# A unit's third and fourth sums, not its first and third, made by accumulating DMAs; a plain block ahead of the first unit; the first norm scaled by columns

## The chip, the cores and the metric

The kernel runs as one program on one core of a Trainium2 chip. Its engines each work through an instruction list of their own, in order, and wait for one another by semaphores: PE (matmuls and transposes), DVE (VectorE), ACT (ScalarE), POOL (GpSimd) and SP, which here only issues DMAs. The metric is the device time of one execution in microseconds (us).

## What is computed

Two layers of a transformer block on x of 256 rows by 1024 columns, float32. Each layer has a gated FFN with 2816 hidden columns, a mixer of three kinds of attention, and a second FFN; a norm stands ahead of each and a last one at the end.

```python
def rms_norm(x, gain):
    y = x * lax.rsqrt(jnp.mean(x * x, axis=-1, keepdims=True) + NORM_EPS)
    return y * gain

def swiglu(h, w_gate, w_up, w_down):
    a, u = h @ w_gate, h @ w_up
    return (jax.nn.silu(a) * u) @ w_down

for l in range(DEPTH):                                   # DEPTH = 2
    x = x + 0.5 * swiglu(rms_norm(x, ffn1_norm[l]), ffn1_w_gate[l], ffn1_w_up[l], ffn1_w_down[l])
    x = x + hybrid_mixer(rms_norm(x, mix_norm[l]), w_in[l], ...)
    x = x + 0.5 * swiglu(rms_norm(x, ffn2_norm[l]), ffn2_w_gate[l], ffn2_w_up[l], ffn2_w_down[l])
return rms_norm(x, final_norm)
```

The change touches the four FFNs (`f1` and `f2` of layers 0 and 1) and the first norm; the mixer stays as it is.

## The kernel before

**Precision.** Every float32 operand of a product is split in two: a high part, rounded by an ACT copy (`high`, L184), and a low part, the rest, by a DVE subtraction (`low`, L187). One product is three matmuls, high by high, high by low and low by high (`mm3`, L175 to L177). So each weight that arrives as `w_r`, `f_G_r` or `f_U_r` is read by ACT, then by DVE, before PE may use it as `w_h` and `w_l`. The normed and transposed x is `f_Th` and `f_Tl`.

**An FFN.** The hidden columns come as blocks of 128. The *first block* (`first_block`, L560) makes blocks 0 and 1 for both row tiles t of 128 rows, 48 matmuls of 128x256 each, gate and up together. When tile 1 begins, it lets DVE and ACT start on the four sums `f_Sh`, `f_Sl` of the quarters of x (`sums`, L614). Its result `f_f_b_h` (silu of gate times up, L554) is transposed on PE into `f_b0tp`. A *plain block* f (`block`, L589) is two steps, `g` and `u`, of 24 matmuls of 128x256 (`f_b`). Blocks 10 to 21 come as two *units* of six: there, gate (G) and up (U) are each computed as one Strassen-Winograd product of 2x2 quarters, with seven products in place of eight (`unit_product`, L641; 12 matmuls of 128x384 each, `f_s`). The seven come in the order `SEVEN`, 1, 5, 6, 3, 7, 2, 4. A *down* step of a block is 12 matmuls of 128x512 (`f_a`).

**The order.** `ffn_steps` (L473) writes one step of `FILL` after each of the 28 products of an FFN: `g` or `u` is half of a plain block, a number is the down step of that block. `REST` and the blocks left over follow. PE, ACT and DVE run in the order in which the program is written; `defer` puts an instruction off by a clock that the program keeps for itself. The order of the DMA issues on SP and POOL comes from the scheduler.

**Weights.** `load` (L307) issues a weight's DMA and its splits. Plain and down weights (512 KB) pass through `w_r`, a ring of 4608 columns, four such loads. A unit's quarter W00, W01, W10 or W11 of 128x4x384 (768 KB) has a tile in a pool of its own. Products 1, 2 and 3 take a quarter as it is (W00, W10, W11); the others take sums of quarters:

- product 5 takes a = W00 + W01: a load of W00 (a second one) and, once it has landed, a DMA from POOL that adds W01 to it in place (L318);
- product 6 takes a + W11, added by DVE in two halves (L344);
- product 7 takes b = W01 + W11, again a load and an accumulating DMA;
- product 4 takes a + W10 (with a as product 6 left it), added by DVE.

For each half of a unit these are 5 loads by SP, 2 accumulating DMAs and 2 adds on DVE. Unit weights are loaded only from the time that the first block is in its tile 1.

**A norm** (`norm`, L398). ACT squares and sums a half row tile (L422), DVE adds the halves (`f_ss`, L428), POOL makes r, one over the root (L429), DVE scales x by r and the gain into `f_xs` (L445), PE transposes that into `f_tp`, ACT makes `f_Th` from it and a second copy `f_xr` in SBUF (`kept`, L464), and DVE takes `f_Tl` from the copy. The sums of the units use the copy too. The first norm is different for tile 1: POOL multiplies x by the gain ahead of time (`f_xg`, L418). Its gain `first_g` is a DMA that writes the 1024 values to all 128 partitions (512 KB). At the start, `WARM` matmuls of zeros (`heat`) run on PE while the first loads are under way.

## Time and profile before

| | us |
|---|---|
| median of three runs | 1311.02 |
| lowest and highest of them | 1310.87, 1311.99 |
| the profiled execution, as timed | 1311.85 |
| its span in the profile | 1310.1 |
| PE busy | 1259.8 (96%) |
| DVE busy | 913.4 (70%) |
| ACT busy | 747.9 (57%) |
| POOL busy | 58.0 (4%) |

The DMAs read 257.95 MB in that span, 198 GB/s, of which the accumulating ones are 25.17 MB. A row of the profile names the line of the kernel, the engine, the operation, and `out<-in` with the names of the tiles; buffer numbers are left out, and `f_` stands for the tiles of all four FFNs. What follows in brackets is the time that the engine stood idle before the instruction, and what ended it. In the table of waits, the figures are the total, the number of times and the longest.

### The profile page before, as it was taken

To read this page: it belongs to the slowest core of one execution; us is meant where nothing else is said; L and a number is where in the kernel's file an instruction comes from. 1 tells how busy PE (TensorE), PEld (TensorE's weight loads), DVE (VectorE), ACT (ScalarE), POOL (GpSimd) and SP (SyncE) were. 2 spreads that over 40 slices of the span, in tenths; PEclk is the share of its full clock that TensorE was granted. 3 is DMA by queue.
4 is the path that set the end of the run, shared out by engine and by line. 5 is a ranking of instruction groups with operands and counts; after the bars stand their busy time and mean duration, and the time that the engine had idled before them with its cause. 6 is when DMAs were issued, how large, how long until landed. Compare 5 with 4: busy or idle time off the path is not lost.

```text
span 1310.1 us, 21172 instructions
## 1 busy us (share of the span) xinstructions
PE 1259.8 (96%) x8280; PEld 1183.3 (90%) x8280; DVE 913.4 (70%) x1354; ACT 747.9 (57%) x1267; POOL 58.0 (4%) x56
## 2 busy tenths in 40 slices
PE   7799999999999989999969999999999999799998
PEld 6799988999999879999869999899999998799996
DVE  5678776765556758797658797677655476688884
ACT  5566656665555546565446565466654654565652
POOL 1000001000000010000000000000000000100000
PEclk8899999999999999999999999999999999899999
DMA  9999755545435678994598994565464466999932
GB/s 282 282 279 263 206 190 162 167 129 147 129 107 178 213 237 215 264 289 154 177 274 210 267 280 158 178 190 150 130 161 121 127 190 177 258 264 271 265 127 82
DMA packets 214885, 260.38 MB, mean 199 GB/s; under 512 B 7425, under 2 KB 198657, under 8 KB 214785
## 3 DMA queue, kind: packets, MB, share of 16 engines
q1 hardware_dynamic: 197600, 233.34, 57.7%
q0 software_dynamic: 16896, 25.17, 11.6%
q8 instruction: 65, 1.06, 0.3%
q10 hardware_dynamic: 288, 0.52, 0.1%
q14 instruction: 36, 0.29, 0.1%
HBM read 257.95 MB, written 1.05 MB: 198 GB/s over the span
## 4 chain that ended last, share of the span: by engine, by line
PE 90%; DMA 5%; DVE 3%; ACT 2%; issue 1%; POOL 0%; SPq 0%; POOLq 0%; DVEq 0%; ACTq 0%
PE f_a L176 6%; PE f_a L177 6%; PE f_a L175 6%; PE f_s L175 6%; PE f_s L177 6%; PE f_s L176 6%; PE f_b L176 5%; PE f_b L175 5%; PE f_b L177 5%; DMA f_G_r<-in_ffn_w_gate 4%; PE mx_ogate L175 4%; PE mx_ogate L176 3%; PE mx_ogate L177 3%; PE mx_odqk L175 2%; PE mx_odqk L177 2%; PE mx_odqk L176 2%
## 5 line engine op out<-in xcount | busy, mean ns | idle before, releaser
L187 DVE TENSOR_TENSOR w_l<-w_r,w_h 128x512 fp32r<-128x512 f32 (+1 forms) x484 | 387.4, 826 | 104.9 <-ACT w_h L184 103.3
L184 ACT ACTIVATE w_h<-w_r 128x512 fp32r<-128x512 f32 (+1 forms) x484 | 344.8, 735 | 94.7 <-PE f_a L176 16.6
L175 PE MATMUL f_b<-f_Th,w_h 128*128 128x256 f32 x512 | 148.4, 290 | 0.0
L176 PE MATMUL f_b<-f_Th,w_l 128*128 128x256 f32 x512 | 148.0, 289 | 0.0
L177 PE MATMUL f_b<-f_Tl,w_h 128*128 128x256 f32 x512 | 147.7, 288 | 0.0
L175 PE MATMUL f_a<-w_h,f_hTh 128*128 128x512 f32 x352 | 139.5, 396 | 0.0
L177 PE MATMUL f_a<-w_l,f_hTh 128*128 128x512 f32 x352 | 139.0, 395 | 0.0
L176 PE MATMUL f_a<-w_h,f_hTl 128*128 128x512 f32 x352 | 138.9, 395 | 0.0
L184 ACT ACTIVATE w_h<-f_G_r 128x1536 fp32r<-128x1536 f32 (+1 forms) x72 | 85.6, 1197 | 60.7 <-DVE f_G_r L344 29.1
L187 DVE TENSOR_TENSOR w_l<-f_U_r,w_h 128x1536 fp32r<-128x1536 f32 (+1 forms) x72 | 100.4, 1399 | 20.1 <-ACT w_h L184 19.9
L175 PE MATMUL mx_ogate<-mx_Th,w_h 128*128 128x256 f32 x384 | 113.0, 294 | 0.0
L176 PE MATMUL mx_ogate<-mx_Th,w_l 128*128 128x256 f32 x384 | 108.6, 283 | 0.6 <-DVE w_l L187 0.6
L187 DVE TENSOR_TENSOR w_l<-f_G_r,w_h 128x1536 fp32r<-128x1536 f32 (+1 forms) x72 | 100.0, 1398 | 12.3 <-ACT w_h L184 11.5
L177 PE MATMUL mx_ogate<-mx_Tl,w_h 128*128 128x256 f32 x384 | 108.5, 283 | 0.0
L184 ACT ACTIVATE w_h<-f_U_r 128x1536 fp32r<-128x1536 f32 (+1 forms) x72 | 85.7, 1196 | 36.0 <-DVE f_U_r L344 22.1
L176 PEld LDWEIGHTS f_b<-f_Th,w_l 128*128 128x128 f32 x512 | 101.1, 197 | 0.2
L177 PEld LDWEIGHTS f_b<-f_Tl,w_h 128*128 128x128 f32 x512 | 101.1, 197 | 0.0
L175 PEld LDWEIGHTS f_b<-f_Th,w_h 128*128 128x128 f32 x512 | 101.1, 197 | 0.0
L175 PE MATMUL f_s<-w_h,f_Sh 128*128 128x384 f32 x256 | 87.2, 341 | 0.0
L177 PE MATMUL f_s<-w_l,f_Sh 128*128 128x384 f32 x256 | 86.6, 338 | 0.0
L176 PE MATMUL f_s<-w_h,f_Sl 128*128 128x384 f32 x256 | 86.6, 338 | 0.0
L177 PEld LDWEIGHTS f_a<-w_l,f_hTh 128*128 128x128 f32 x352 | 66.1, 188 | 15.8
(265 smaller groups left out, 2933.5 us busy)
## 6 DMA issues: line engine op xcount, KB each, us to landing
w_r<-in_ffn_w_down SPq DMA_DIRECT2D x88, 512.0 KB, 4.3
w_r<-in_w_in SPq DMA_DIRECT2D x84, 512.0 KB, 3.9
f_G_r<-in_ffn_w_gate SPq DMA_DIRECT2D x40, 768.0 KB, 8.1
f_U_r<-in_ffn_w_up SPq DMA_DIRECT2D x40, 768.0 KB, 7.3
w_r<-in_ffn_w_gate SPq DMA_DIRECT2D x40, 512.0 KB, 5.7
w_r<-in_ffn_w_up SPq DMA_DIRECT2D x40, 512.0 KB, 6.8
f_G_r<-in_ffn_w_gate POOLq DMA_DIRECT2D x16, 768.0 KB, 10.1
f_U_r<-in_ffn_w_up POOLq DMA_DIRECT2D x16, 768.0 KB, 10.2
```

The costliest lines, as they stand in the source:

```text
L175: nc.tensor.matmul(o, sh, mh, start=first, stop=False, skip_group_check=again)
L176: nc.tensor.matmul(o, sl, mh, start=False, stop=False, skip_group_check=again)
L177: nc.tensor.matmul(o, sh, ml, start=False, stop=last, skip_group_check=again)
L184: nc.scalar.activation(hi, src, AF.Copy)
L187: nc.vector.tensor_tensor(lo, src, hi.bitcast(F32), op=ALU.subtract)
```

## The change

- **Unit weights.** The four quarters are each loaded once: a = W00, b = W01, c = W11, d = W10. Product 1 takes a. For product 5 DVE adds b to a, for product 6 DVE adds c to a. Behind product 6's issue an accumulating DMA adds W11 to b, which is then product 7's; behind product 3's an accumulating DMA adds W10 to a, which is then product 4's. Products 3 and 2 take c and d. Per half of a unit: 4 loads by SP, 2 accumulating DMAs, 2 adds on DVE.
- **Order.** `LEAD` puts both steps of plain block 2 ahead of product 1 of the first unit; `FILL` and `REST` are shifted to make up for it. The work is the same in all.
- **First norm.** The gain comes as 8 rows of 128 (`gain_rows`); PE transposes them behind the heat, DVE copies the result to `gain_cols` (128x8). x is scaled by r alone, and DVE multiplies by the gain after the transposes, which leaves `f_xr` in SBUF; `f_Th` and `f_Tl` are made from that. The DMA of `first_g` and POOL's `f_xg` are gone; the DMAs of the gain and of `ident` are issued by ACT.
- **Other FFN norms.** `f_Tl` is taken from the transposes in PSUM, and ACT's copy for the sums is made later.
- `WARM` is 9 instead of 6.

```diff
-FILL = "gugu0 1gu2 3gu4 g", "u5 gu10 11 gu12 13 gu14 15 "
-REST = 6, 7, 8, 9
+LEAD = "gu"
+FILL = "gu0 1 gu2 3 gu4 5 gu", "gu6 gu7 10 gu11 12 13 14 15"
+REST = 8, 9
 FIRST, SINGLE, UNIT0 = 2, 8, 10
 SLOPES = [2.0 ** (-8.0 * (i + 1) / N_ALIBI) for i in range(N_ALIBI)]
 CHUNK = 1024
 PIECE = 512
 SCR = 2048
 ORDERED = {mybir.EngineType.PE, mybir.EngineType.Activation, mybir.EngineType.DVE}
-WARM = 6
+WARM = 9
 RING = 6656
 RAW = 4608
 PACE = 2.3 / 1024
...
-    def transpose(o, src):
-        nc.tensor.transpose(o, src, ident)
+    def transpose(o, src, n=P):
+        nc.tensor.transpose(o, src, ident[:n, :n])
         spend(0.11)
...
-    steps = {1: ((("q1", (0, 0)),), None, "q1"), 5: ((("a", (0, 0), (0, 1)),), None, "a"), 6: ((("q2", (1, 1)),), ("a", "q2"), "a"),
-             3: ((), None, "q2"), 7: ((("b", (0, 1), (1, 1)),), None, "b"), 2: ((("q3", (1, 0)),), None, "q3"), 4: ((), ("a", "q3"), "a")}
+    steps = {1: (("a", (0, 0)), None, "a", None), 5: (("b", (0, 1)), ("a", "b"), "a", None), 6: (("c", (1, 1)), ("a", "c"), "a", ("b", (1, 1))),
+             3: (None, None, "c", ("a", (1, 0))), 7: (None, None, "b", None), 2: (("d", (1, 0)), None, "d", None), 4: (None, None, "a", None)}
     unit_places = {}
...
         j = len(jobs)
-        loads, add, source = steps[p]
-        loads = [(tag, [w[i * 512:(i + 1) * 512, c0 + h * UC:c0 + (h + 1) * UC].rearrange("(k p) n -> p k n", p=P) for i, h in q]) for tag, *q in loads]
+        def quarter(x):
+            if x:
+                tag, (i, h) = x
+                return tag, w[i * 512:(i + 1) * 512, c0 + h * UC:c0 + (h + 1) * UC].rearrange("(k p) n -> p k n", p=P)
+        new, add, source, more = steps[p]
         jobs.append({"name": f"{name}_{p}", "n": 4 * UC, "own": None, "whole": True,
-                     "unit": (unit_places.setdefault(name, {}), loads, add, source)})
+                     "unit": (unit_places.setdefault(name, {}), quarter(new), add, source, quarter(more))})
         uses[j] = 4
         for k in range(4):
             where[name, p, k] = j, k * UC, UC
...
         if "unit" in job:
-            places, parts, add, source = job["unit"]
-            for tag, srcs in parts:
-                places[tag] = raw_place("raw" + tag[0], unit_pool[0], 1 if tag == "b" else 2, [P, 4 * UC], f"{name}_r", j)
-                to = places[tag][0].rearrange("p (k n) -> p k n", k=4)
-                nc.sync.dma_start(to, srcs[0])
-                for src in srcs[1:]:
-                    nc.gpsimd.dma_start(to, src, accum_op=ALU.add)
-            for t in {source, *(add or ())}:
+            places, new, add, source, more = job["unit"]
+            if new:
+                tag, src = new
+                places[tag] = raw_place("raw" + tag, unit_pool[0], 2 if tag == "a" else 1, [P, 4 * UC], f"{name}_r", j)
+                nc.sync.dma_start(places[tag][0].rearrange("p (k n) -> p k n", k=4), src)
+            for t in {source, *(add or ()), *(more or ())[:1]}:
                 for i in places[t][1]:
                     if i in loaded:
                         loaded[i][2]()
                 if places[t][1][-1] != j:
                     places[t][1].append(j)
+            if more:
+                tag, src = more
+                nc.gpsimd.dma_start(places[tag][0].rearrange("p (k n) -> p k n", k=4), src, accum_op=ALU.add)
             raw = places[source][0]
             if add:
                 to, other = [places[t][0] for t in add]
...
-    def norm(name, gain_src, gain=None, last=None, ahead={}):
+    def norm(name, gain_src, last=None, gain_cols=None):
...
             if "g" not in st:
-                g = gain or gain_tile(gain_src, D, f"{name}_g", "gain")
-                st["g"] = [g[:, half_cols(i)] for i in range(2)]
+                g = gain_cols is None and gain_tile(gain_src, D, f"{name}_g", "gain")
+                st["g"] = g and [g[:, half_cols(i)] for i in range(2)]
                 if last is None:
                     nT[name] = transposed(name)
             if h == 0:
-                if last is not None or t in ahead:
+                if last is not None:
                     st["xg", t] = row_tile(f"{name}_xg{t}")
                 if last is not None and t == 0:
                     st["sq"] = row_tile(f"{name}_sq")
                 st[t] = st["sq"] if last is not None else row_tile(f"{name}_xs{t}"), small.tile([P, 2], F32, tag="ss", name=f"{name}_ss{t}"), \
                     small.tile([P, 1], F32, tag="rstd", name=f"{name}_r{t}")
             defer(0.7, lambda: square(t, h))
-            if last is not None or t in ahead:
-                ahead.get(t, nc.vector).tensor_tensor(st["xg", t][:, half_cols(h)], x[t][:, half_cols(h)], st["g"][h], op=ALU.mult)
+            if last is not None:
+                nc.vector.tensor_tensor(st["xg", t][:, half_cols(h)], x[t][:, half_cols(h)], st["g"][h], op=ALU.mult)
...
             for h in range(2):
-                if t in ahead:
-                    nc.vector.tensor_scalar(xs[:, half_cols(h)], st["xg", t][:, half_cols(h)], r, None, op0=ALU.mult)
+                if gain_cols is not None:
+                    nc.vector.tensor_scalar(xs[:, half_cols(h)], x[t][:, half_cols(h)], r, None, op0=ALU.mult)
                 else:
                     nc.vector.scalar_tensor_tensor(xs[:, half_cols(h)], x[t][:, half_cols(h)], r, st["g"][h], op0=ALU.mult, op1=ALU.mult)
                 defer(0.8 + 0.7 * h, lambda h=h: turn(t, h))
...
             th, tl = nT[name]
-            high(th[:, h * 4:h * 4 + 4, rows(t)], tp)
             src = tp
             if name[0] == "f":
                 if h == 0:
                     kept[name, t] = row_tile(f"{name}_xr{t}").rearrange("p (k s) -> p k s", s=P)
-                src = kept[name, t][:, h * 4:h * 4 + 4, :]
-                nc.scalar.activation(src, tp, AF.Copy)
-            low(tl[:, h * 4:h * 4 + 4, rows(t)], src, th[:, h * 4:h * 4 + 4, rows(t)])
+                if gain_cols is not None:
+                    src = kept[name, t][:, h * 4:h * 4 + 4, :]
+                    nc.vector.tensor_tensor(src, tp, gain_cols[:, h * 4:h * 4 + 4, None].to_broadcast([P, 4, P]), op=ALU.mult)
+                    made.add((name, "kept", t, h))
+            split(th[:, h * 4:h * 4 + 4, rows(t)], tl[:, h * 4:h * 4 + 4, rows(t)], src)
+            if name[0] == "f" and gain_cols is None:
+                defer(1.5, lambda: (nc.scalar.activation(kept[name, t][:, h * 4:h * 4 + 4, :], tp, AF.Copy), made.add((name, "kept", t, h))))
             made.add((name, t, h))
             if t == 1 and h == 1:
                 table(AF.Exp if name.startswith("mx") else AF.Silu)
...
         steps, single = [], {"g": FIRST, "u": FIRST}
-        for u in range(UNITS):
-            fill = []
-            for w in FILL[u].replace("g", " g ").replace("u", " u ").split():
+        def others(text):
+            for w in text.replace("g", " g ").replace("u", " u ").split():
                 if w in single:
-                    fill.append(("B", w, single[w]))
+                    yield "B", w, single[w]
                     single[w] += 1
                 else:
-                    fill.append(("D", int(w)))
+                    yield "D", int(w)
+        steps += others(LEAD)
+        for u in range(UNITS):
+            fill = list(others(FILL[u]))
             for i, what in enumerate("GU"):
                 for j, p in enumerate(SEVEN):
                     steps.append(("P", u, what, p))
...
             def sums():
-                need(*[(name, t, h) for t in range(NT) for h in range(2)])
+                need(*[(name, "kept", t, h) for t in range(NT) for h in range(2)])
                 (a11, a12), (a21, a22) = [[kept[name, t][:, 4 * h:4 * h + 4, :] for h in range(2)] for t in range(NT)]
                 tt, stt = nc.vector.tensor_tensor, nc.vector.scalar_tensor_tensor
                 todo = [lambda: tt(a22, a22, a21, op=ALU.subtract), lambda: tt(a21, a11, a21, op=ALU.subtract),
...
     x_in(0)
-    first_gain = gain_tile(a["ffn1_norm"][0], D, "first_g", "gain")
-    nc.sync.dma_start(ident, c["eye"])
+    gain_rows = small.tile([KT, P], F32, tag="gr", name="gain_rows", bufs=1)
+    nc.scalar.dma_start(gain_rows, a["ffn1_norm"][0].rearrange("(k p) -> k p", p=P))
+    nc.scalar.dma_start(ident, c["eye"])
     table(AF.Square)
     heat = acc_bank("heat")
     for _ in range(WARM):
         nc.tensor.matmul(heat[:, :256], zeros[:, :P], zeros, start=True, stop=True)
-    first = norm("f1_0", None, first_gain, ahead={1: nc.gpsimd})
+    gain_bank = tp_bank("gain_tp")
+    transpose(gain_bank[:, 0, :KT], gain_rows, KT)
+    gain_cols = small.tile([P, KT], F32, tag="gc", name="gain_cols", bufs=1)
+    nc.vector.tensor_copy(gain_cols, gain_bank[:, 0, :KT])
+    first = norm("f1_0", None, gain_cols=gain_cols)
     first(0, 0)
     first(0, 1)
     need(("f1_0", 0, 0))
```

DVE, first FFN of layer 0, from the last of the first three sums (`f_xr`, L619 before and L633 now) to the low part of product 5's weight. `f_b_h` ends with the number of the bank it is from; `f_Sl` is a sum's low part; `G_1_r` and `G_5_r` are tiles of unit weights, which the change calls by the product that loads them. Before:

```order
L619 SCALAR_TENSOR_TENSOR f_0_xr_115<-f_0_xr_217,f_0_xr_115 128x512
L187 TENSOR_TENSOR w_l<-f_0_G_1_r,w_h 128x1536
L187 TENSOR_TENSOR w_l<-w_r,w_h 128x1024
L620 SCALAR_TENSOR_TENSOR f_0_xr_115<-f_0_xr_115 128x512
L187 TENSOR_TENSOR f_0_Sl<-f_0_xr_217,f_0_Sh 128x512
L554 TENSOR_TENSOR f_0_f_0_b_h<-f_0_f_0_b_s,f_0_b_238 128x256
L187 TENSOR_TENSOR f_0_Sl<-f_0_xr_115,f_0_Sh 128x512 x2
L187 TENSOR_TENSOR w_l<-f_0_G_5_r,w_h 128x1536
```

and now:

```order
L633 SCALAR_TENSOR_TENSOR f_0_xr_121<-f_0_xr_223,f_0_xr_121 128x512
L188 TENSOR_TENSOR w_l<-f_0_G_1_r,w_h 128x1536
L188 TENSOR_TENSOR w_l<-w_r,w_h 128x1024
L634 SCALAR_TENSOR_TENSOR f_0_xr_121<-f_0_xr_121 128x512
L188 TENSOR_TENSOR f_0_Sl<-f_0_xr_223,f_0_Sh 128x512
L351 TENSOR_TENSOR f_0_G_1_r<-f_0_G_1_r,f_0_G_5_r 128x768
L568 TENSOR_TENSOR f_0_f_0_b_h<-f_0_f_0_b_s,f_0_b_248 128x256
L188 TENSOR_TENSOR f_0_Sl<-f_0_xr_121,f_0_Sh 128x512
L351 TENSOR_TENSOR f_0_G_1_r<-f_0_G_1_r,f_0_G_5_r 128x768
L188 TENSOR_TENSOR f_0_Sl<-f_0_xr_121,f_0_Sh 128x512
L188 TENSOR_TENSOR f_0_hTl_145<-f_0_b0tp_351,f_0_hTh_144 128x2x128
```

One half of the add of b to a (L351) now stands ahead of `f_f_b_h`, the other behind it.

PE, the same FFN, around the transposes `f_b0tp` of tile 1 of the first block. `b_331` before, and `b_319` now, is the bank of plain block 2; `s_135` that of product 1. Before:

```order
L177 MATMUL f_0_s_135<-w_l,f_0_Th 128x384
L175 MATMUL f_0_b_331<-f_0_Th,w_h 128x256
L176 MATMUL f_0_b_331<-f_0_Th,w_l 128x256
L177 MATMUL f_0_b_331<-f_0_Tl,w_h 128x256
L169 MATMUL f_0_b0tp_335<-ident,f_0_f_0_b_h 128x128 x2
L175 MATMUL f_0_b_331<-f_0_Th,w_h 128x256
```

and now, where the transposes stand behind 21 of the 48 matmuls of `b_319`, and product 1 comes after the last of them:

```order
L176 MATMUL f_0_b_319<-f_0_Th,w_h 128x256
L177 MATMUL f_0_b_319<-f_0_Th,w_l 128x256
L178 MATMUL f_0_b_319<-f_0_Tl,w_h 128x256
L170 MATMUL f_0_b0tp_351<-ident,f_0_f_0_b_h 128x128 x2
L176 MATMUL f_0_b_319<-f_0_Th,w_h 128x256
```

Behind the transposes stood 21 matmuls of a plain half and then product 5; now there are 27 of the plain block, product 1 and a plain half (24) between them and product 5.

DVE at the start of the program, from its two memsets to the second low part of x's transposed tile 0. `tp` are the transposes. Before:

```order
L1164 MEMSET zeros 128x256
L428 SCALAR_TENSOR_TENSOR f_0_ss_101<-f_0_ss_101 128x1
L445 SCALAR_TENSOR_TENSOR f_0_xs_100<-x_72,f_0_r_102,first_g 128x512 x2
L187 TENSOR_TENSOR f_0_Tl<-f_0_xr_115,f_0_Th 128x4x128
L187 TENSOR_TENSOR w_l<-w_r,w_h 128x512
L187 TENSOR_TENSOR f_0_Tl<-f_0_xr_115,f_0_Th 128x4x128
```

and now:

```order
L1178 MEMSET zeros 128x256
L1190 COPY gain_cols<-gain_tp 128x8
L435 SCALAR_TENSOR_TENSOR f_0_ss_108<-f_0_ss_108 128x1
L450 TENSOR_SCALAR f_0_xs_107<-x_72,f_0_r_109 128x512 x2
L471 TENSOR_TENSOR f_0_xr_121<-f_0_tp_116,gain_cols 128x512
L188 TENSOR_TENSOR f_0_Tl<-f_0_xr_121,f_0_Th 128x4x128
L188 TENSOR_TENSOR w_l<-w_r,w_h 128x512
L471 TENSOR_TENSOR f_0_xr_121<-f_0_tp_129,gain_cols 128x512
L188 TENSOR_TENSOR f_0_Tl<-f_0_xr_121,f_0_Th 128x4x128
```

The copy of the gain stands ahead of `f_ss`, and a multiplication is added ahead of each low part.

## The prediction

> **What bounds the kernel now.** First the top of the page, to see which engine sets the time; then PE's waits, longest first; then the chain that ended last, at the place of the longest wait.
>
> ```profile
> span 1310.1 us, 21172 instructions
> ...
> PE 1259.8 (96%) x8280; PEld 1183.3 (90%) x8280; DVE 913.4 (70%) x1354; ACT 747.9 (57%) x1267; POOL 58.0 (4%) x56
> ...
> PE f_b0tp L169 <- DVE f_f_b_h L554: 27.7, 4, 8.5
> PE f_s L177 <- DVE w_l L187: 4.3, 4, 1.1
> PE f_tp L169 <- DVE f_xs L445: 3.8, 2, 3.0
> ...
> PE f_b L176 <- DVE f_Tl L187: 0.6, 2, 0.3
> ```
>
> PE is busy 96% of the span, and the change leaves its matmuls as many as they are, but for three of `heat` and one small transpose at the start. So the time can change only where PE waits or runs on a slow clock. More than half of all its waiting is one row: four waits, 27.7 us, one in each FFN, where the transposes of `f_b0tp` want `f_f_b_h` from DVE. DVE is not slow there; this is the chain in the first FFN:
>
> ```profile
> 27.36 11.39 DMA f_G_r<-in_ffn_w_gate
> ...
> 38.84 0.16 ACT w_h L184
> ```
>
> An accumulating DMA for product 5 is issued only when its base has landed (27.36), lands 11.39 us later, and ACT, which works in order, stands at 38.84 before its split. Behind ACT's split stand the `f_Sh` splits, behind them DVE's `f_Sl`, behind it `f_f_b_h`, and PE waits for that. Here are, in PE's timeline, for each of the four FFNs: the first matmul of the first unit (the end T of the first block), the transposes with their wait, and the first matmul of product 5.
>
> ```profile
> 29.47 0.34 PE L175 MATMUL f_s<-w_h,f_Th 128*128 128x384 f32 x1
> ...
> 33.01 0.28 PE L176 MATMUL f_b<-f_Th,w_l 128*128 128x256 f32 x1
> 33.13 0.28 PE L177 MATMUL f_b<-f_Tl,w_h 128*128 128x256 f32 x1
> ...
> 41.95 0.69 PE L169 MATMUL f_b0tp<-ident,f_f_b_h 128*128 128x128 f32 x2 [8.54 <-DVE f_f_b_h L554]
> 46.90 0.34 PE L175 MATMUL f_s<-w_h,f_Sh 128*128 128x384 f32 x1
> ...
> 482.31 0.34 PE L175 MATMUL f_s<-w_h,f_Th 128*128 128x384 f32 x1
> 482.49 0.34 PE L176 MATMUL f_s<-w_h,f_Tl 128*128 128x384 f32 x1
> ...
> 491.29 0.69 PE L169 MATMUL f_b0tp<-ident,f_f_b_h 128*128 128x128 f32 x2 [5.02 <-DVE f_f_b_h L554]
> 495.27 0.34 PE L175 MATMUL f_s<-w_h,f_Sh 128*128 128x384 f32 x1
> ...
> 674.09 0.34 PE L175 MATMUL f_s<-w_h,f_Th 128*128 128x384 f32 x1
> 686.40 0.69 PE L169 MATMUL f_b0tp<-ident,f_f_b_h 128*128 128x128 f32 x2 [8.38 <-DVE f_f_b_h L554]
> 691.37 0.52 PE L175 MATMUL f_s<-w_h,f_Sh 128*128 128x384 f32 x1
> ...
> 1124.72 0.34 PE L175 MATMUL f_s<-w_h,f_Th 128*128 128x384 f32 x1
> 1134.37 0.69 PE L169 MATMUL f_b0tp<-ident,f_f_b_h 128*128 128x128 f32 x2 [5.71 <-DVE f_f_b_h L554]
> 1139.25 0.34 PE L175 MATMUL f_s<-w_h,f_Sh 128*128 128x384 f32 x1
> ```
>
> Matmuls overlap, so the step from one start to the next is what counts: 0.12 us for 128x256 (33.01 to 33.13) and 0.175 for 128x384 (482.31 to 482.49). Between the transposes and product 5 stand 21 matmuls of a plain half: at full clock 0.2 + 21 × 0.12 = 2.7 us, but the four took 4.95, 3.98, 4.97 and 4.88. So each wait has a tail of a slow clock, 2.2, 1.3, 2.3 and 2.2 us, 7.9 together. Waits at `f_b0tp`, waits in product 1 (`f_s`, 4.3) and tails make about 40 us.
>
> **The change, part by part.**
>
> *Product 5 without an accumulating DMA, and a plain block ahead.* Now b is a plain load, DVE adds it to a, and 48 matmuls (5.76 us) of g2 and u2 stand between T and product 1: PE runs 21 of them, then the transposes, then 27, product 1, g3, product 5. The new wait is found from DVE's list; these are its durations in the second FFN of layer 0:
>
> ```profile
> 482.09 1.75 DVE L187 TENSOR_TENSOR w_l<-f_G_r,w_h 128x1536 fp32r<-128x1536 f32 x1
> 483.76 1.22 DVE L187 TENSOR_TENSOR w_l<-w_r,w_h 128x1024 fp32r<-128x1024 f32 x1
> ...
> 490.21 0.69 DVE L187 TENSOR_TENSOR f_Sl<-f_xr,f_Sh 128x512 fp32r<-128x512 f32 x1 [4.64 <-ACT f_Sh L184]
> 490.82 0.42 DVE L554 TENSOR_TENSOR f_f_b_h<-f_f_b_s,f_b 128x256 f32<-128x256 f32 x1
> ...
> 496.10 1.82 DVE L344 TENSOR_TENSOR f_G_r<-f_G_r,f_G_r 128x768 f32<-128x768 f32 x2
> ```
>
> Starts on DVE lie 0.06 to 0.09 closer than durations. DVE's list from T − 0.2: low part of G_1 (1.67), of g3 (1.14), the fourth sum and one `f_Sl` (0.61 to 0.69 each, as the 128x512 row), and new in front of `f_f_b_h` one half of the add (0.91). `f_f_b_h` then starts at T + 4.8, and PE's transposes 0.47 later (490.82 to 491.29): T + 5.2. PE is there at T + 2.5. So **the wait is not removed, it shrinks to 2.7 us**, and it is DVE's list that ends last, no longer a DMA. From there: transposes 0.2, 27 × 0.12 = 3.24, product 1 12 × 0.175 = 2.1, g3 24 × 0.12 = 2.9: product 5 starts at T + 13.6, with 5.76 us of work more behind PE than at the same point before. The wait of 1.07 in product 1 is gone, since its low part is ready 10 us ahead. I take the clock as full throughout.
>
> So the gain of an FFN is (product 5 before) + 5.76 − (new T + 13.6). T itself moves, as follows.
>
> *The start.* These rows carry it; the last two are issue to landing, in the first 30 us and over the whole run.
>
> ```profile
> 1.22 5.16 PE L1171 MATMUL heat<-zeros 128*128 128x256 f32 x12 [1.22 <-DVE zeros L1164]
> 6.05 0.55 POOL L429 TENSOR_TENSOR f_r<-f_ss,mhalf 128x1 f32<-128x1 f32 x1 [5.60 <-DVE f_ss L428]
> 8.54 1.42 DVE L445 SCALAR_TENSOR_TENSOR f_xs<-x,f_r,first_g 128x512 f32<-128x512 f32 x2 [2.58 <-DMA first_g<-in_ffn_norm]
> 9.35 1.97 PE L169 MATMUL f_tp<-ident,f_xs 128*128 128x128 f32 x8 [2.97 <-DVE f_xs L445]
> ...
> 16.34 0.37 SPq L337 DMA_DIRECT2D w_r<-in_ffn_w_gate  x1
> ...
> w_r<-in_ffn_w_gate SPq DMA_DIRECT2D x4, 512.0 KB, 8.0
> ...
> w_r<-in_ffn_w_down SPq DMA_DIRECT2D x88, 512.0 KB, 4.3
> ```
>
> The wait for the gain's DMA (2.58) goes. But PE transposes `gain_rows` only behind the heat, whose 9 matmuls at 5.16 / 6 = 0.86 end at 9.0, and DVE copies `gain_cols` ahead of `f_ss`, which it had ready to do at 5.8. The 128x8 transpose and copy are in no row; a 128x128 transpose takes 0.25 (1.97 / 8) and DVE's smallest copies here some 0.2 to 0.4, so 0 to 0.7 together; I take 0.4. With `f_ss`, r (0.55) and their hand-overs, `f_xs` starts near 10.2 and the transposes near 10.75 instead of 9.35: **+1.4**. From the first half's transposes (11.35) DVE then has, up to the first low part of tile 1: three multiplies by `gain_cols`, three low parts `f_Tl` and eight `w_l`, of 0.69 each like the 128x512 row above (9.7); g2's low part (1.2); `f_ss`, r and `f_xs` (1.8 with hand-overs); three waits for ACT's high parts, some 0.6 each: 14.5 us, to 25.9. g2's own load is issued only when a part of the ring is free (16.34 before, about 17.3 now), and ACT's high part of it stands ahead of those of tile 1. If it lands after 5 us, between 4.3 and 8.0, that adds 1.2. Then come 48 matmuls of tile 1 at 0.12, of which the first few want only the high part (some 0.4 earlier). So T comes to 31.3 if g2 is never waited for, 35.5 if it takes 8.0; I take **32.5**, 3.0 later. Gain 46.90 + 5.76 − 46.1 = **6.6** (3.6 to 7.8).
>
> *Second FFN, layer 0.* T gains the 0.28 of a wait for `f_Tl`, which now reads the transposes directly instead of a copy that ACT makes first: 495.27 + 5.76 − (482.03 + 13.6) = **5.4**. *Second FFN, layer 1*, the same: 1139.25 + 5.76 − (1124.44 + 13.6) = **7.0**.
>
> *First FFN, layer 1.*
>
> ```profile
> 665.62 0.63 PE L169 MATMUL f_tp<-ident,f_xs 128*128 128x128 f32 x4 [0.88 <-DVE f_xs L445]
> ```
>
> PE waits here for the last norm, and the new block puts a high part of 1.05 between ACT's two squares and a low part of 1.22 ahead of DVE's `f_xs`: the transposes come up to 1.3 later, T with them (bounds 0 and 2.5, if the second low part counts as well). Two slow first matmuls of product 5 (0.28 together) go too: 691.37 + 0.28 + 5.76 − (675.4 + 13.6) = **8.4** (7.2 to 9.7).
>
> *The rest, at nothing.* One accumulating DMA now serves product 7 and one product 4:
>
> ```profile
> f_U_r<-in_ffn_w_up POOLq DMA_DIRECT2D x16, 768.0 KB, 10.2
> ```
>
> Product 7 starts three products and three plain halves after product 5: 3 × 2.1 + 3 × 2.9 = 15 us; the DMA goes out when the add of product 5 has read b, some 4 us before product 5, and needs 10.2 plus 3 us of splitting. Product 4 has two more steps of each. So PE's work hides both, by 5 us and more. DVE adds for products 5 and 6 instead of 6 and 4: as many. The 12.6 MB fewer (16 quarters) take nothing off PE. Were the cover gone by 1 us in each of the 16 halves, it would cost 16 us.
>
> **Sum**: 6.6 + 5.4 + 8.4 + 7.0 = 27.4 us, 2.1%. The profiled execution took 1311.85 (its span is 1310.1), 0.8 above the median of 1311.02; 1311.85 − 27.4 = 1284.5, and from the median 1283.6. I say 1284.
>
> **The rivals.**
>
> *The clock drops in the new waits.* Windows of the granted clock (the column behind the five engines):
>
> ```profile
> 9.00:9.50 0.50, 0.15 (x1) 0.15 (x2) 0.50 (x2) 0.00 (x0) 0.00 (x0) 0.82 1.10 375
> ...
> 36.00:37.00 1.00, 0.00 (x0) 0.00 (x0) 0.00 (x0) 0.00 (x0) 0.00 (x0) 0.81 1.10 264
> 40.00:41.00 1.00, 0.00 (x0) 0.00 (x0) 0.13 (x1) 1.00 (x3) 0.33 (x1) 0.50 1.04 397
> ```
>
> The clock falls to 0.50. A mean of 0.82 over 9.0 to 9.5 puts the fall at 9.3, 2.9 us after the heat's end (1.22 + 5.16); 0.81 over 36 to 37 puts it at 36.6, 3.2 after the stop (41.95 − 8.54). A wait of 2.7 stays under both, by little. If it drops in all four, the old tails of 7.9 stay: 1292. Chance 0.15. The Trainium skill ("TensorE: Matmul & The Clock Gate", Part 1: The HAM clock gate) has the clock halved after an idle window of 3.4 us that runs free of the kernel; by that rule a wait of 2.7 never holds a whole window and this rival would be out. The fall after 2.9 us is shorter than its window, so the trace does not grant that, and the chance stays.
>
> *The start is no later than before* (g2 hidden, the gain's chain short): T stays at 29.5, 3 us more: 1281. Chance 0.15.
>
> *DVE becomes the bound inside the FFNs*: both adds now stand in one stretch, products 5 and 6, at 1.82 each. Against it: DVE is at 70%, and as many adds as before. A wait of 1 us in each of 16 halves: 1300. Chance 0.08.
>
> *The change doesn't do what it says*: b lands late, and `f_f_b_h` comes no earlier, so that the transposes stay at T + 12.5, 9.0, 12.3 and 9.7. From them to product 5 there are then 0.2 + 3.2 + 2.1 + 2.9 = 8.4 us, of which 5.76 is work that comes later now, in place of 4.95, 3.98, 4.97 and 4.88: 2.3, 1.3, 2.3 and 2.2 us gained, less 4.3 for the later T: 1308. Chance 0.04.
>
> *Slower*: the accumulating DMA of product 7 is late. It waits for DVE's add, so it cannot go out early, and ACT would stand at its split with everything behind it, as for product 5 now, but in all 16 halves instead of 4. It decides from about 17 us between add and landing, against 10.2 measured; 3 us a half give 48 − 27: 1332. Chance 0.03.
>
> **How the numbers follow.** The forecast, 1284, has 0.55, and its own bounds (start −1.2 to +3.0, layer 1 −1.3 to +1.2) make 1281 to 1289. With the clock on one side, the early start on the other: 1278 to 1296, which leaves out the last three, 0.15. A measurement of this kernel can tell some 0.2%, 2.6 us, from no change: faster 0.93, same 0.03, slower 0.04.
>
> **What would show it.** Right: `f_b0tp` waits of 2 to 3 us, four times, for `f_f_b_h`, with DVE busy in the time before; no ACT wait on a DMA of `f_G_r`; the granted clock full from T on; no `f_s` wait in product 1; T near 32.5 in the first FFN. Wrong: waits on a gate or up quarter at products 7 or 4; a clock of 0.5 behind the new waits; PE waiting in the halves for `w_l`; T of the first FFN past 36, with ACT waiting for g2.

## The result and the profile after

The changed kernel took 1291.05 us (median; 1290.84 to 1292.58) beside 1311.51 for the kernel before. The ratio is 0.9844 with a 95% interval of 0.9827 to 0.9861: 20.5 us less, where 27.4 were forecast. The time lies inside the range of 1278 to 1296, but 2 us above the 1281 to 1289 that the forecast's own bounds gave.

The page of the changed kernel, its two lines on the span and PE, and the first two rows of PE's waits:

```profile
span 1289.3 us, 21216 instructions
...
PE 1257.9 (98%) x8287; PEld 1181.5 (92%) x8287; DVE 914.2 (71%) x1359; ACT 750.1 (58%) x1263; POOL 55.5 (4%) x54
...
PE f_b0tp L170 <- DVE f_f_b_h L568: 10.1, 4, 2.5
PE f_b L176 <- DVE f_f_b_h L568: 2.6, 2, 1.3
```

The four waits at `f_b0tp` fell from 27.7 to 10.1 us, 2.5 each, and the row of `f_s` with four waits of 1.07 in product 1 is gone. In its place stands a row that was not there before: a plain half `f_b` waits for `f_f_b_h`. Here is PE's timeline of the changed kernel, for the four FFNs in turn: in the first the end T of the first block (the first matmul of plain block 2), the transposes, product 1, the plain half behind it, and product 5; in the others the transposes, product 1 and product 5, and in the third FFN one more row.

```profile
32.15 0.28 PE L176 MATMUL f_b<-f_Th,w_h 128*128 128x256 f32 x1
37.28 0.44 PE L170 MATMUL f_b0tp<-ident,f_f_b_h 128*128 128x128 f32 x2 [2.45 <-DVE f_f_b_h L568]
40.79 0.34 PE L176 MATMUL f_s<-w_h,f_Th 128*128 128x384 f32 x1
44.35 0.39 PE L176 MATMUL f_b<-f_Th,w_h 128*128 128x256 f32 x1 [1.32 <-DVE f_f_b_h L568]
47.33 0.34 PE L176 MATMUL f_s<-w_h,f_Sh 128*128 128x384 f32 x1
...
481.74 0.41 PE L170 MATMUL f_b0tp<-ident,f_f_b_h 128*128 128x128 f32 x2 [2.54 <-DVE f_f_b_h L568]
486.70 0.34 PE L176 MATMUL f_s<-w_h,f_Th 128*128 128x384 f32 x1
491.70 0.34 PE L176 MATMUL f_s<-w_h,f_Sh 128*128 128x384 f32 x1
...
670.82 0.66 PE L170 MATMUL f_b0tp<-ident,f_f_b_h 128*128 128x128 f32 x2 [2.54 <-DVE f_f_b_h L568]
675.69 0.34 PE L176 MATMUL f_s<-w_h,f_Th 128*128 128x384 f32 x1
680.64 0.34 PE L176 MATMUL f_s<-w_h,f_Sh 128*128 128x384 f32 x1
749.72 0.39 PE L176 MATMUL f_b<-f_Th,w_h 128*128 128x256 f32 x1 [1.25 <-DVE f_f_b_h L568]
...
1114.20 0.57 PE L170 MATMUL f_b0tp<-ident,f_f_b_h 128*128 128x128 f32 x2 [2.54 <-DVE f_f_b_h L568]
1119.18 0.34 PE L176 MATMUL f_s<-w_h,f_Th 128*128 128x384 f32 x1
1124.16 0.34 PE L176 MATMUL f_s<-w_h,f_Sh 128*128 128x384 f32 x1
```

In the first FFN product 1 follows the transposes by 3.51 us, as at a full clock, and then the plain half waits 1.32. In the other three it follows by 4.96, 4.87 and 4.98, and no plain half waits behind it before product 5. The granted clock (the column behind the five engines' busy shares) tells why:

```profile
37.00:38.00 1.00, 0.72 (x6) 0.72 (x7) 1.00 (x3) 1.00 (x2) 0.00 (x0) 1.00 0.97 280
482.00:483.00 1.00, 1.00 (x11) 1.00 (x10) 1.00 (x3) 1.00 (x3) 0.00 (x0) 0.92 0.40 118
483.00:484.00 1.00, 1.00 (x6) 1.00 (x6) 1.00 (x4) 0.93 (x3) 0.20 (x1) 0.50 0.00 0
670.00:671.00 1.00, 0.18 (x1) 0.22 (x2) 1.00 (x3) 0.57 (x1) 0.00 (x0) 0.79 1.04 313
1114.00:1115.00 1.00, 0.80 (x5) 0.84 (x6) 1.00 (x3) 0.86 (x2) 0.00 (x0) 0.65 0.86 259
```

It stayed full there in the first FFN and fell to 0.50 in the other three. By these four product-5 starts, with 5.76 us of plain work more done, the FFNs gained 5.3, 4.0, 7.2 and 4.4 us (the last is less the 1.25 us wait at 749.72): 20.9 in all; the spans of the two profiles differ by 20.8.

### The profile page after: what moved, and what is told of

The parts are those of the page before. It is cut to its first block, busy times and chain, and to the rows that moved or that the text cites. A ratio compares the mean times of both kernels' runs of the same rounds, so it can differ in the third digit from the quotient of the medians.

```text
span 1289.3 us, 21216 instructions
## 1 busy us (share of the span) xinstructions
PE 1257.9 (98%) x8287; PEld 1181.5 (92%) x8287; DVE 914.2 (71%) x1359; ACT 750.1 (58%) x1263; POOL 55.5 (4%) x54
## 4 chain that ended last, share of the span: by engine, by line
PE 90%; DVE 5%; ACT 1%; DMA 1%; issue 1%; POOL 0%; SPq 0%; POOLq 0%; DVEq 0%; ACTq 0%
PE f_a L178 6%; PE f_a L177 6%; PE f_a L176 6%; PE f_s L176 6%; PE f_s L178 6%; PE f_s L177 6%; PE f_b L177 5%; PE f_b L176 5%; PE f_b L178 5%; PE mx_ogate L176 4%; PE mx_ogate L178 3%; PE mx_ogate L177 3%; DVE w_l L188 2%; PE mx_odqk L176 2%; PE mx_odqk L177 2%; PE mx_odqk L178 2%
## 5 line engine op out<-in xcount | busy, mean ns | idle before, releaser
L188 DVE TENSOR_TENSOR w_l<-f_U_r,w_h 128x1536 fp32r<-128x1536 f32 (+1 forms) x72 | 100.1, 1399 | 32.5 <-ACT w_h L185 31.0
```

Of the source, the lines that this page charges most:

```text
L188: nc.vector.tensor_tensor(lo, src, hi.bitcast(F32), op=ALU.subtract)
```

## The experiments

Two theories stood at the start. **A**: the gain is the accumulating DMA taken out from in front of ACT, and what ends last now is DVE's list; the plain block covers nothing that this list leaves open. **B**: the plain block is what covers the wait. For the tails of the slow clock, **C**: they are time lost; **D**: they only hide the wait for `f_f_b_h` that stands behind them.

**1. Without the plain block (e1).** The changed kernel with the order of before.

```diff
-LEAD = "gu"
+LEAD = ""
-FILL = "gu0 1 gu2 3 gu4 5 gu", "gu6 gu7 10 gu11 12 13 14 15"
-REST = 8, 9
+FILL = "gugu0 1gu2 3gu4 g", "u5 gu10 11 gu12 13 gu14 15 "
+REST = 6, 7, 8, 9
```

> The changed kernel with LEAD, FILL and REST as before, so without the plain block ahead of the first unit. Theory A (the gain is the accumulating DMA taken out from in front of ACT; DVE's list from the end T of the first block to product 5 ends last, and the plain block covers nothing that this list leaves open): product 5 starts at about T + 9 instead of T + 15.1 with 5.76 us of plain work ahead of it, so every FFN gains 0 to 0.5 us more, and the waits for a plain block's f_f_b_h right behind product 1 (1.3 us each, twice) and the plain weights ahead of tile 1 in the first FFN go: 1284 to 1289 us. f_b0tp waits about 1.4 us, and product 5 waits for w_l about 1 us. Theory B (the plain block is what covers the wait): each FFN loses most of 5.76 us against the changed kernel, 1305 to 1312 us, with f_b0tp waits of 5 us and more.

1289.85 us (1289.42 to 1291.70), ratio 0.9837 [0.9822, 0.9851]: no slower than with the block, so B falls; but it is also above the 1284 to 1289 that A had given. Its PE timeline in the first FFN, at T, product 5 and the wait in it:

```profile
31.06 0.34 PE L176 MATMUL f_s<-w_h,f_Th 128*128 128x384 f32 x1
...
38.96 0.34 PE L176 MATMUL f_s<-w_h,f_Sh 128*128 128x384 f32 x1
...
40.06 0.44 PE L178 MATMUL f_s<-w_l,f_Sh 128*128 128x384 f32 x1 [0.58 <-DVE w_l L188]
```

Product 5 starts at T + 7.9, earlier than the T + 9 foreseen. But from there to an FFN's last product on the sums the four FFNs took 125.1 us each, against 122.3 in the second and fourth FFN of the changed kernel: DVE is still behind, and PE waits for `w_l` later, at the first unit's product 5 and the second plain half behind it and at the second unit's product 5. The block ahead neither costs nor brings much by itself; it moves the place where PE meets DVE's list.

**2. The plain block alone (e2).** The kernel before, with only `LEAD`, `FILL` and `REST` of the change.

> The kernel before with only LEAD, FILL and REST of the change: accumulating DMAs still make products 5 and 7. Theory A: the four waits at f_b0tp stay, since the DMA in front of ACT stays (5 to 10 us each), and behind the transposes product 1 and a plain half wait their turn; a gain of 0 to 8 us, 1303 to 1312 us. Theory B: most of the gain, 1290 to 1297 us.

1313.42 us (1311.49 to 1314.60), ratio 1.0013 [1.0003, 1.0022]: nothing gained, and above the 1303 to 1312 that A had given as well. PE's two longest waits, and ACT's split of product 5's weight in the first FFN with PE's wait behind it:

```profile
PE f_b L176 <- DVE f_f_b_h L558: 26.0, 4, 11.7
PE f_b0tp L170 <- DVE f_f_b_h L558: 7.0, 5, 1.7
...
43.18 1.48 ACT L185 ACTIVATE w_h<-f_G_r 128x1536 fp32r<-128x1536 f32 x1 [11.49 <-DMA f_G_r<-in_ffn_w_gate]
...
52.37 0.58 PE L176 MATMUL f_b<-f_Th,w_h 128*128 128x256 f32 x1 [11.72 <-DVE f_f_b_h L558]
```

The expectation that the waits stay at `f_b0tp` was wrong in its place: there they are short, and the same late weight holds up the `f_f_b_h` of the plain block instead. The two rows make 33 us. B falls a second time.

**3. The unit weights alone (e6).** The kernel before with `steps`, `plan_product` and `load` of the change and nothing else.

> The kernel before with only the unit weights of the change (four loads, accumulating DMAs for products 7 and 4, adds for 5 and 6); order, norms and heat as before. If these alone make the gain: 1287 to 1291 us, at or below the changed kernel, with f_b0tp waits of 1 to 2 us. If the plain block or the norms have a share: 1294 us or more.

1291.77 us (1291.09 to 1292.70), ratio 0.9853 [0.9838, 0.9868]. This part alone makes 19 of the 20.5 us, 0.8 us above the 1287 to 1291 expected. Its waits at `f_b0tp`, and its T in the first FFN:

```profile
PE f_b0tp L169 <- DVE f_f_b_h L559: 4.6, 4, 1.2
...
28.97 0.34 PE L175 MATMUL f_s<-w_h,f_Th 128*128 128x384 f32 x1
```

**4. The old weights, another order on ACT (e5).** The kernel before, where the splits of one weight in each FFN are issued only when PE's program reaches it.

```diff
-        for m in range(total - 1, -1, -1):
-            defer(size * (total - 1 - m), lambda m=m: until(m))
-        until(total - 1)
+        if not name.endswith("G0_5"):
+            for m in range(total - 1, -1, -1):
+                defer(size * (total - 1 - m), lambda m=m: until(m))
+            until(total - 1)
```

> The kernel before, accumulating DMAs and all, with one thing moved: the splits of product 5 of the first unit's gate half (one in each FFN) are issued only when PE's program reaches that product, so ACT makes the f_Sh and the silu ahead of them. Theory A1 (it is the place in ACT's order that costs: the late weight held up everything behind it): the four waits at f_b0tp go (27.7 us to under 4), and a shorter wait for w_h and w_l at product 5 itself takes their place, since the weight still lands 6 to 10 us after T: product 5 at about T + 13, 10, 13 and 10.5 instead of 17.4, 13.0, 17.3 and 14.5, a gain of 12 to 20 us: 1292 to 1300 us. Theory A2 (the landing itself sets product 5, wherever ACT waits): the waits only change their name, 1307 to 1312 us.

1297.51 us (1295.51 to 1300.43), ratio 0.9901 [0.9881, 0.9920], with every accumulating DMA still in place:

```profile
PE f_s L177 <- DVE w_l L187: 9.3, 8, 1.5
PE f_s L175 <- ACT w_h L184: 6.5, 4, 2.8
...
PE f_b0tp L169 <- DVE f_f_b_h L555: 1.2, 4, 0.3
```

The waits at `f_b0tp` are gone, and product 5 itself waits 1.6 us on average for its high part. ACT waits for the DMA of a gate quarter still, four times, 7.1 us in all, where it was 28.6. So 13 of the 19 us of e6 come from the weight's place in ACT's order alone, with the accumulating DMAs all in place. The other 6 are about what PE still waits for the high part, 6.5; that they go with the late landing is argued from this, for e6 also loads 16 quarters fewer, and no run takes the two apart.

**5. Idle matmuls in the wait (e4).** The changed kernel, with four matmuls of zeros right ahead of the transposes (x8 in the profile, which counts each of them twice).

```diff
+HOLD = 4
...
                         tp = tp_bank(f"{name}_b0tp{t}")
+                        if t:
+                            for _ in range(HOLD):
+                                nc.tensor.matmul(tp[:, 2:4, :], zeros[:, :P], zeros, start=True, stop=True)
```

> The changed kernel with 4 idle matmuls of zeros (128x256) on PE right ahead of the transposes f_b0tp of tile 1, in each FFN, about 1.9 us of the 2.5 us wait. The clock then stays full in all four. Theory C (the tails of a slow clock, 1.5 us in three FFNs, are time lost): 1286 to 1287.5 us. Theory D (behind them stands DVE's list, which lets f_f_b_h of the plain block out at T + 12.2 whatever PE does; the tail only hides that wait): the wait of the next plain half, 1.2 to 1.3 us, that only the first FFN shows, appears in the other three too: 1290 to 1291 us.

1291.27 us (1290.69 to 1291.46): nothing won, and 0.3 above what D had given. PE in the second FFN, with the zeros, the transposes, product 1 and the plain half:

```profile
479.40 1.89 PE L595 MATMUL f_b0tp<-zeros 128*128 128x256 f32 x8
482.01 0.44 PE L171 MATMUL f_b0tp<-ident,f_f_b_h 128*128 128x128 f32 x2 [0.72 <-DVE f_f_b_h L569]
485.51 0.34 PE L177 MATMUL f_s<-w_h,f_Th 128*128 128x384 f32 x1
489.08 0.39 PE L177 MATMUL f_b<-f_Th,w_h 128*128 128x256 f32 x1 [1.32 <-DVE f_f_b_h L569]
```

The clock is held (3.50 us from transposes to product 1, in all four FFNs), and the wait of 1.32 that only the first FFN had appears in the second and fourth too, with 0.45 in the third. Theory D: behind PE stands DVE. From the transposes to product 5 the changed kernel takes 9.96 us with the tail (481.74 to 491.70) and 10.05 in the first FFN without one (37.28 to 47.33): there the tail costs nothing of its own. The third FFN is the exception: 9.82 with the tail, and 9.18 with the idle matmuls (671.10 to 680.28), so that its tail costs 0.6 us.

**6. Fewer operations in front (e8, e9).** If DVE's list is the bound, taking three of its operations out of the way must help. The fourth sum and the `f_Sl` of products 3 and 7 are put off, first without the plain block (by 6.0), then in the changed kernel (by 9.0).

```diff
-                    defer(0.8 * i, fn)
+                    defer(0.8 * i + (LATE if i in (3, 6, 7) else 0.0), fn)
```

> The changed kernel without the plain block ahead, and with the fourth sum and the f_Sl of products 3 and 7 (three DVE operations of 0.6 us) put off until behind product 5's splits. If DVE's list from T to product 5 is what ends last: 0.6 us off the wait at f_b0tp and up to 1.2 us more off that of product 5, 4 to 7 us in four FFNs against the kernel without the plain block (1289.85): 1283 to 1286.5 us. If something else ends last there (ACT's splits, a landing): 1288.5 to 1290.5 us.

> The changed kernel, plain block ahead and all, with the fourth sum and the f_Sl of products 3 and 7 put off until behind the plain block's f_f_b_h. If it is DVE's list that lets that f_f_b_h out only at T + 12.2, it now comes three operations of 0.6 us earlier, near T + 10.4; the f_b0tp wait falls from 2.5 to about 1.9 us, the clock stays full, the next plain half waits 0 to 0.4 us, and product 5 starts near T + 13.5 instead of T + 15.0 in each FFN: 5 to 7 us less than the changed kernel (1291.05), 1284 to 1286 us. If the three operations are only paid later, as without the plain block: 1289 to 1291 us, with new waits for w_l at products 5 and 6.

Without the block: 1289.23 us (1287.92 to 1290.37), against 1289.85: a miss. Product 5 of the first unit no longer waits, but product 6 then waits 0.92 us for `w_l` in each FFN; the operations are paid there. With the block: 1286.81 us (1285.31 to 1288.67), ratio 0.9819 [0.9806, 0.9833], 4.2 less than the changed kernel and 2.4 less than the late operations without the block, though the last two runs overlap (from 1287.92 to 1288.67). The profiles agree: from T to the end of an FFN's last product on the sums e8 takes 133.0 us, and e9 137.1 in three of the four, with 5.76 us of plain work more in it. Here the block ahead does work, as cover for DVE. It is short of the 5 to 7 expected, and in its profile, of the slowest of the four executions (1288.67), the clock fell in all four FFNs. The second of them, in PE's timeline, and a window of the clock behind its wait:

```profile
480.50 0.41 PE L171 MATMUL f_b0tp<-ident,f_f_b_h 128*128 128x128 f32 x2 [1.94 <-DVE f_f_b_h L569]
485.46 0.34 PE L177 MATMUL f_s<-w_h,f_Th 128*128 128x384 f32 x1
...
490.44 0.34 PE L177 MATMUL f_s<-w_h,f_Sh 128*128 128x384 f32 x1
...
481.00:482.00 1.00, 1.00 (x9) 1.00 (x8) 1.00 (x2) 0.41 (x2) 0.00 (x0) 0.69 0.71 214
```

From the transposes to product 5 it took 9.94 us; in the three FFNs of e10 whose clock stayed full, 8.75 to 8.84. With DVE's list shortened, a tail costs 1.1 to 1.2 us.

**7. Product 4 on DVE (e7).** A third add in each half instead of the second accumulating DMA.

```diff
-             3: (None, None, "c", ("a", (1, 0))), 7: (None, None, "b", None), 2: (("d", (1, 0)), None, "d", None), 4: (None, None, "a", None)}
+             3: (None, None, "c", None), 7: (None, None, "b", None), 2: (("d", (1, 0)), None, "d", None), 4: (None, ("a", "d"), "a", None)}
```

> The changed kernel with product 4's sum made by DVE (a + d, as before) instead of by an accumulating DMA: DVE adds three times in each of the 16 halves, 16 x 1.82 = 29 us more of DVE, and 12.6 MB fewer pass through POOL's queue. If DVE has room inside the halves: 1290 to 1292 us. If DVE is the bound there (a rival in the prediction), 1 to 1.8 us in each half: 1305 to 1320 us, with waits for w_l in the halves.

1289.46 us (1288.52 to 1290.09), ratio 0.9834 [0.9819, 0.9849]: 29 us more on DVE cost nothing. If anything it is 1.6 faster, and its profile lacks the 1.25 us wait at the seam of the two units. Of the profiles with the block ahead and the change's unit weights, the four whose product 4 comes from an accumulating DMA have that wait (the changed kernel, e3, e4, e9: 1.24 to 1.26) and the four that add on DVE have not (e7, e10, e11, e12). DVE is the bound at the head of an FFN and has room in the halves.

**8. The old first norm (e3).** The changed kernel with the first norm as before and 6 heat matmuls.

> The changed kernel with the first norm as before (first_g by DMA, POOL's multiplication, ACT's copies in the first FFN) and 6 heat matmuls. If the start of the change is worth what its parts look like (transposes at 8.84 instead of 9.35, no contention with POOL), the first block ends 0.5 to 2 us later than in the changed kernel: 1291.5 to 1293 us. If the multiplications on DVE cost as much as they save, within 0.5 us of the changed kernel: 1290.5 to 1291.5. If the scaling by columns is a loss (four multiplications of 0.69 and the ping-pong with ACT, 4 us on the way of the first FFN): 1288 to 1290 us.

1290.41 us (1289.32 to 1291.10), within scatter of the changed kernel. In PE's timeline T of the first FFN is 31.45 with the old norm and 32.15 with the new one. One such pair proves little: with the new norm and no block ahead, T is 31.06 in e1 and 29.57 in e8, which differ in three late operations of DVE alone.

**9. Put together (e10, e11, e12).** Late sums and product 4 on DVE; then the old first norm and 6 heat matmuls as well; then three idle matmuls in the wait.

> The same, with product 4's sum made by DVE as well. The changed kernel with that alone took 1289.46. If the two add up: 1.5 us below the run with the late sums alone, 1282.5 to 1284.5 us. If the 1.5 us was scatter: the same as that run within 0.7 us.

> The same again, with the first norm and the heat as before the change. The first block of the first FFN ended at 28.97 us with the old norm and at 31.06 with the scaling by columns where no plain block was ahead, and some 0.7 us apart with it. If that holds: 0.5 to 1.5 us below the run with late sums and product 4 on DVE. If the old norm's T is bound by the same waits for the plain block's weight: within 0.4 us of it.

> The run with late sums, product 4 on DVE and the old first norm (1281.9), with 3 idle matmuls of zeros (1.4 us) on PE in the 1.9 us wait ahead of f_b0tp. There, two of the four FFNs of the profile had a tail of a slow clock behind a wait of 1.9 us: 4.97 us from the transposes to product 1 and 4.96 from there to product 5, against 3.48 and 5.27 in the two without; so a tail costs 1.2 us now that DVE's list is shorter. If the idle matmuls hold the clock: no tail in any of the four, 3.5 and 5.3 us, and 1279 to 1281 us. If the list on DVE still stands behind it, as with the changed kernel and its idle matmuls: 1281.5 to 1282.5 us.

| | us | lowest to highest | ratio, 95% interval |
|---|---|---|---|
| late sums, product 4 on DVE (e10) | 1285.43 | 1283.28 to 1286.42 | 0.9806 [0.9792, 0.9819] |
| and the old first norm (e11) | 1281.90 | 1281.09 to 1283.14 | 0.9783 [0.9770, 0.9797] |
| and idle matmuls (e12) | 1280.90 | 1278.99 to 1282.04 | 0.9770 [0.9757, 0.9783] |

The first step is 1.4 us, as two parts that add up, though its runs overlap with those of e9. The second is 3.5 us, more than the 0.5 to 1.5 expected. T of the first FFN went from 31.84 to 30.08, 1.8 us, but the two profiled executions differ by 1.6 only (1283.28 and 1281.71), so the rest of the 3.5 lies between executions that no profile shows and isn't explained. The third, 1.0 us, lies inside the scatter; no FFN of its profile has a tail (3.5 us each from the transposes to product 1), as expected, but its gain isn't settled. All three lie below every run of the changed kernel, and the last two over 2% below the kernel before.

## Why the prediction was right, and where it was off

**What bounds the kernel, and the removal: right.** The four waits were the accumulated weight in front of ACT's other work; e6 shows that this part alone makes 19 of the 20.5 us, e5 that the place in the order is two thirds of them.

**The new wait: right.** 2.7 us were worked out from DVE's list, 2.5 were measured, and the transposes came at T + 5.13 in the first FFN and T + 5.22 in the others, for the T + 5.2 of the forecast.

**The way from the transposes to product 5: here the size was off.** The step "27 × 0.12, product 1, g3: product 5 at T + 13.6" left out that the plain half behind product 1 takes the same bank as plain block 2, whose `f_f_b_h` DVE must first have made. DVE's rows in the first FFN:

```profile
35.94 0.95 DVE L351 TENSOR_TENSOR f_G_r<-f_G_r,f_G_r 128x768 f32<-128x768 f32 x1
36.81 0.41 DVE L568 TENSOR_TENSOR f_f_b_h<-f_f_b_s,f_b 128x256 f32<-128x256 f32 x1
...
43.02 0.94 DVE L351 TENSOR_TENSOR f_G_r<-f_G_r,f_G_r 128x768 f32<-128x768 f32 x1
43.89 0.41 DVE L568 TENSOR_TENSOR f_f_b_h<-f_f_b_s,f_b 128x256 f32<-128x256 f32 x1
```

I followed DVE's list to the first `f_f_b_h` (36.81) and not on to the second (43.89), with no gap between. The list lets the plain half start at T + 12.2 in the first FFN, not T + 10.7; product 5 then starts at T + 15.0 to T + 15.2 instead of T + 13.6. That is 1.4 to 1.6 us in each FFN, 6.2 together. With the 1.25 of the next point, and T some 1 us earlier in all than I had it, this makes the 6.5 us between 27.4 and 20.9. The forecast's own bounds had no term for it, so they missed; the wider range, which was made for the clock and the early start, holds the time by luck.

**At nothing, "The rest": one miss.** The same pattern, a plain block, product 1, the next plain half, stands at the seam of the two units too, and cost 1.25 us once, at 749.72. Otherwise the halves hide everything as forecast: no split of a gate or up quarter waits for its DMA, e7 shows room on DVE, and the accumulating DMAs landed in 8.2 and 7.8 us.

**The rival of the clock: it came in three of four, and cost next to nothing of its own.** I gave it 0.15 and 7.9 us. The clock fell in waits of 2.5 us, a sign that I had named as one of being wrong, and e4 shows that DVE's list would have taken nearly all of that time anyway. "I take the clock as full throughout" was wrong, and so was the price: not 7.9 us but 0.6, as long as DVE's list stands behind. That the time came within 1 us of this rival's 1292 is chance: the 6.2 us above are DVE's, not the clock's.

**The start: T right by luck, by two errors that cancel.** 32.5 forecast, 32.15 measured. The heat was to end at 9.0 and the transposes to come at 10.75:

```profile
1.22 5.99 PE L1186 MATMUL heat<-zeros 128*128 128x256 f32 x18 [1.22 <-DVE zeros L1178]
...
8.84 1.09 PE L170 MATMUL f_tp<-ident,f_xs 128*128 128x128 f32 x8 [1.48 <-DVE f_xs L450]
...
19.72 1.06 ACT L185 ACTIVATE w_h<-w_r 128x1024 fp32r<-128x1024 f32 x1 [2.42 <-DMA w_r<-in_ffn_w_gate]
```

Nine heat matmuls end at 7.2. The profile counts two passes for each; they start 0.43 us apart up to 4.8 and 0.22 apart from 5.1 on, as the clock rises, so that 0.86 was the price of one at the slow clock and the last ones cost half. When the clock rises differs from one execution to the next: in the seven profiles with nine heat matmuls they end between 6.9 and 8.4. The 1.9 us won here went into waits of DVE and ACT for one another at the new multiplication, and into ACT's wait for the plain block's weight, 2.42 us (worked out: some 1.2 on T, from a landing of 5 us; it landed in 4.8). What the new norm does to T can be said roughly only. Without the block ahead T is 28.97 to 29.47 in three profiles with the old norm (the kernel before, e5, e6), and 29.57 and 31.06 with the new one (e8, e1). With the block it is 30.08 to 31.45 in four with the old norm (e2, e3, e11, e12), and 31.84 to 32.53 in five with the new one. So the new norm loses some 1 to 1.5 us there on average.

**The other FFNs' T: right.** The second FFN of each layer came some 0.5 earlier (0.28 forecast), layer 1's first one some 0.8 later (1.3). No run takes the change of those norms by itself.

**The other rivals.** The start did come later than before (32.15 for 29.47), and "Slower" and "DVE the bound in the halves" did not come. "The change doesn't do what it says" is out too: no ACT split waits for a unit weight's DMA any more.

## What to carry to other kernels

A late operand costs more than its own lateness where an engine works in order: everything written behind its first reader waits too, and moving that reader behind the work that is ready can be worth most of the gain. When a wait is removed, follow the list of the engine that then ends last until it has nothing left to hand over, not just to the first thing that is waited for. A cover helps only where there is work to move behind it: with the new unit weights, neither the plain block ahead nor three operations put off brought anything clear of scatter alone (1291.05 and 1289.23, against 1289.85 in e1 with neither), and both together brought 3.0 us (1286.81).

## What the runs showed of the hardware

**The granted clock falls after waits far shorter than those of the kernel before.** In six profiles with waits of 1.84 to 2.54 us at `f_b0tp` (the changed kernel, e3, e7, e9, e10, e11) it fell behind 15 of the 24; behind the eight waits of 0.54 to 0.72 of e4 and e12, never. In the changed kernel's second FFN, PE stopped at 479.20 and resumed at 481.74, and the mean of 0.92 puts the fall at 482.84: 3.6 us after the stop, 1.1 after the work had begun again. In the third it fell near 670.58, 2.3 us after the stop; in e9 near 481.38, 0.9 after PE had resumed from a wait of 1.94. The prediction took 2.9 us as the shortest; it is not a bound. The Trainium skill ("TensorE: Matmul & The Clock Gate", Part 1: The HAM clock gate) names an idle window of 3.4 us that runs free of the kernel. The grid below agrees with that length, but by these rows PE need not be idle for all of it: a wait of 1.9 us can be enough.

**What decides is where the wait lies.** In the changed kernel the clock falls at 482.84, 670.58 and 1114.30 (a mean of 0.65 over 1114 to 1115) and is back at 486.26 (0.87 over 486 to 487). So half speed lasts 3.42 us here, and the falls lie 187.7 and 443.7 us apart, 55 and 130 times 3.413: the clock changes at the marks of a grid here. The first number behind the length is PE's busy time:

```profile
32.28:35.70 3.42, 2.55 (x22) 2.34 (x20) 3.42 (x4) 1.67 (x4) 0.00 (x0) 1.00 0.90 327
35.70:39.11 3.41, 1.83 (x16) 1.83 (x16) 3.41 (x6) 2.38 (x5) 0.09 (x1) 1.00 0.86 270
479.43:482.84 3.41, 1.10 (x10) 1.14 (x11) 3.41 (x6) 2.12 (x4) 0.00 (x0) 1.00 0.53 154
486.00:487.00 1.00, 1.00 (x8) 1.00 (x8) 1.00 (x2) 0.04 (x1) 0.00 (x0) 0.87 0.81 91
```

In the second FFN one step of the grid holds 2.31 us of PE's wait, and the clock falls at its end. In the first FFN a mark at 35.70 divides a wait of nearly the same length into 0.87 and 1.58 us, and the clock stays. It is so in all 24 cases: ahead of each of the 15 falls lies a step with 1.85 to 2.54 us idle, and in the nine others no step has more than 1.74. The border is not the same everywhere: in the first block of the first FFN a step with 1.51 us idle (22.04 to 25.46, 1.91 busy) was enough. So a wait of 2 us isn't safe or unsafe by its length alone. The 2.9 and 3.2 us that the prediction took from the kernel before are times from a stop of PE to the next mark; they say where on the grid PE stopped, and not how long it may stop.
